# Stick-breaking attention tiles worked in their PSUM bank, without GpSimd

## The chip, the cores and the metric
The kernel runs on one core of a Trainium2 chip. The metric is the device time of one execution in microseconds (us). TensorE multiplies matrices, VectorE and ScalarE do elementwise work, GpSimd too, and SyncE starts the transfers. SBUF is the on-chip memory; PSUM holds the results of TensorE in eight banks of 512 fp32 columns by 128 partitions.

## The reference
Two blocks are run one after the other on a sequence of 512 tokens of width 1024. The first has a state-space layer, a latent-attention layer and a gated feed-forward after each. The second has two layers that project the input into three kinds of heads and gate and mix their outputs. The change touches the second block: the stick-breaking heads, and the rotation of the queries and keys of the differential heads.

```python
def _partial_rope(t, cos, sin):
    x1 = t[..., :half]; x2 = t[..., half:ROT_DIM]
    r1 = x1 * cos - x2 * sin
    r2 = x2 * cos + x1 * sin
    return jnp.concatenate([r1, r2, t[..., ROT_DIM:]], axis=-1)

# stick-breaking heads, one block of 128 queries
strict = kpos[None, :] < qpos[:, None]
z = jnp.einsum('bhqd,bhkd->bhqk', qb, k) * HEAD_DIM ** -0.5
log_fail = jnp.where(strict, jax.nn.log_sigmoid(-z), 0.0)
after = lax.cumsum(log_fail, axis=3, reverse=True) - log_fail
weights = jnp.where(strict, jnp.exp(jax.nn.log_sigmoid(z) + after), 0.0)
o = jnp.einsum('bhqk,bhkd->bhqd', weights, v)
```

## The kernel before
**Matrix products.** Most weights are fp32 and are split into a high and a low half of a faster format: ScalarE copies the raw weights into the high half (`wh`), VectorE subtracts to get the low half (`wl`); a product is then three matmuls. In the trace all tiles of a pool share a name: `wr_r`, `wh_r` and `wl_r` are raw, high and low weights; `bl` and `bh` hold the working tiles of the second block; `bank` is any PSUM bank; `x`, `xh_r`, `xl_r` are the hidden state and its halves.

**The order of work** is not the program order. The class `Plan` records every instruction of the whole kernel with an assumed cost, its dependences and a lag, and sorts them: a list scheduler runs forward and backward over all of the work twelve times and the order with the earliest modelled end is emitted. Each engine then executes its queue in that fixed order and waits where an operand is late. All instructions are issued from line 263, so every row of the trace names that line. The costs that matter here, in us for n columns (lines 175 to 197):

```python
t = 0.068 + n / 960.0                       # VectorE
if name == "tensor_scalar" and out.space != PSUM and n > 64 and ...:
    t = 0.12 + n / 1920.0                   # VectorE, all in SBUF
elif name == "affine_select":
    t = 0.05 + n * 0.0015                   # GpSimd
else:
    t = 0.15 + n * 0.0021                   # GpSimd, two tensors
```

**The second block's layer** (`block2_layer`) has 8 units of stick-breaking heads, then 16 of differential heads and 8 of forgetting heads. A unit is a pair of heads and a block of 128 queries. Between the units, as work for TensorE while the others run the elementwise steps, stand projections: queries, keys and values of later units (the table `before`, lines 2047 to 2053). During the units the banks are divided: two for projections (`g`), three for scores (`s`), two for transposes (`t`), one for outputs (`o`), each used in rotation.

A unit of stick-breaking heads (`attend_c`, line 1913) handles two heads (`e`). For each it multiplies queries and keys into a score bank, n = 128 to 512 columns, as far as the block's last key, and then makes the weights. With softplus(z) = max(z, ln(1 + exp(min(z, 30)))), a weight is the exponential of z minus the sum of softplus from the right up to its own column. Two GpSimd selects on the diagonal 128 columns keep the strict order: one sets softplus to zero there before the scan, one the weight after the exponential. The weights are transposed on TensorE, copied to SBUF and multiplied by the values.

The rotation (`roped`, line 1836) copies a projection out of its bank with a scale, exchanges rows by a VectorE shuffle, multiplies the exchanged copy by sines on GpSimd and the copy by cosines on VectorE, and adds. `split_q` and `split_k` then make high and low halves of queries and keys; for the differential heads' keys the subtraction in `split_k` runs on GpSimd.

Of the kernel before, what the change touches and what calls it, by code (L numbers as in the profile page):

```python
# [12 lines left out]
F32 = mybir.dt.float32  # L13
# [3 lines left out]
AF = mybir.ActivationFunctionType  # L17
ALU = mybir.AluOpType
AX = mybir.AxisListType

P = 128
D = 1024
S = 512
# [16 lines left out]
NEG = -1e30  # L40
# [486 lines left out]
class Net:  # L527
# [804 lines left out]

    def load_mask(self, pool):

        self.mask = pool.tile([P, S], F32, name="mask")
        self.nc.sync.dma_start(self.mask, self.A["mask"])

    def softmax_exp(self, e, p, i, sm):

        nc = self.nc  # L1340
        n = (i + 1) * P
        mx = self.small(1, "mx", 8)
        nc.vector.tensor_tensor_reduce(e[:, :n], p[:, :n], self.mask[:, S - n :], -1.0, 3e38, ALU.add, ALU.min, accum_out=mx)
        nc.scalar.activation(e[:, :n], e[:, :n], AF.Exp, scale=-1.0, bias=mx, accum_out=sm)
        return e

# [432 lines left out]
    def block2_layer(self, bp, l, hs, start):  # L1779
        nc, A = self.nc, self.A  # L1780
        V, G, SC = nc.vector, nc.gpsimd, nc.scalar
        wf, wv = A[f"w_in2f{l}"], A[f"w_in2v{l}"]
        tk = lambda: bp.tile([P, S], F32, tag="tk", bufs=7)
# [29 lines left out]
        def split_q(src, sc):  # L1813
            t = [qk(), qk()]
            for e, r in enumerate(halves):
                SC.activation(t[e][r], src[r], AF.Copy, scale=sc)
                V.scalar_tensor_tensor(t[e][halves[1 - e]], src[r], sc, t[e][r], ALU.mult, ALU.subtract)
            return t

        def split_k(src, E):  # L1820
            t, low = [qk(), qk()], [qk(), qk()]
            for e, r in enumerate(halves):
                for to in (r, halves[1 - e]):
                    SC.activation(t[e][to], src[r], AF.Copy)
                E.tensor_tensor(low[e][r], src[r], t[e][r], ALU.subtract)
                SC.activation(low[e][halves[1 - e]], low[e][r], AF.Copy)
            return t + low

        def scores2(q, k, e, i):
            n, d = (i + 1) * P, slice(i * P, (i + 1) * P)  # L1830
            p = self.psum("s")
            nc.tensor.matmul(p[:, :n], q[e][:, d], k[e][:, :n], start=True, stop=False)
            nc.tensor.matmul(p[:, :n], q[e][:, d], k[2 + e][:, :n], start=False, stop=True)
            return p

        def roped(name, j, sc):
            p = fm(name, j)
            x, sw = rk(), rk()
            SC.activation(x, p, AF.Copy, scale=sc)
            V.stream_shuffle(sw, x, [i + 8 if i < 8 else i - 8 if i < 16 else i for i in range(32)])  # L1840
            G.tensor_tensor(sw, sw, self.sin2, ALU.mult)
            V.tensor_tensor(x, x, self.cos2, ALU.mult)
            V.tensor_tensor(x, x, sw, ALU.add)
            return x

# [14 lines left out]
        qa, ka, qc, kc, qb, kb = ({} for _ in range(6))  # L1860
# [38 lines left out]
        def values(pr, i, pts, blk):  # L1899

            if i == 0:
                outs[pr] = self.psum("o")
            po = outs[pr]
            for j in range(i + 1):
                for e in range(2):
                    at = (2 * pr + e) * 64
                    nc.tensor.matmul(po[64 * e : 64 * e + 64, i * P : (i + 1) * P], vt[blk][:, j, at : at + 64],
                                     pts[e][:, j * P : (j + 1) * P], start=j == 0, stop=j == i,
                                     tile_position=(0, 64 * e))
            return outs.pop(pr) if i == NB - 1 else None  # L1910


        def attend_c(pr, i):
            n, d = (i + 1) * P, slice(i * P, (i + 1) * P)
            pts = []
            for e in range(2):
                p = scores2(qc[pr], kc[pr], e, i)
                z, sp = tk(), tk()
                SC.activation(z[:, :n], p[:, :n], AF.Copy)
                V.tensor_scalar(sp[:, :n], z[:, :n], 30.0, None, ALU.min)  # L1920
                SC.activation(sp[:, :n], sp[:, :n], AF.Exp)
                SC.activation(sp[:, :n], sp[:, :n], AF.Ln, bias=1.0)
                V.tensor_tensor(sp[:, :n], sp[:, :n], z[:, :n], ALU.max)
                G.affine_select(sp[:, d], sp[:, d], pattern=[[-1, P]], compare_op=ALU.is_gt, fill=0.0, base=0,
                                channel_multiplier=1)
                V.tensor_tensor_scan(sp[:, :n][:, ::-1], self.ones.to_broadcast([P, n]), sp[:, :n][:, ::-1], 0.0,
                                     ALU.mult, ALU.add)
                G.tensor_tensor(z[:, :n], z[:, :n], sp[:, :n], ALU.subtract)
                SC.activation(z[:, :n], z[:, :n], AF.Exp)
                G.affine_select(z[:, d], z[:, d], pattern=[[-1, P]], compare_op=ALU.is_gt, fill=0.0, base=0,  # L1930
                                channel_multiplier=1)
                pts.append(self.transp(bp, z, i, e))
            po = values(pr, i, pts, 3)
            if po is not None:
                V.tensor_tensor(gc[pr], po, gc[pr], ALU.mult)
# [95 lines left out]
            kc[1] = split_k(fm("ck", 1), V)  # L2031

        def aq(h):
            qa[h] = split_q(roped("aq", h, 0.125), 1.0)

        def ak(h):
            ka[h] = split_k(roped("ak", h, 1.0), G)

        def bk1():
            forget_k(1)  # L2040
# [2 lines left out]
            for h in range(4):  # L2043
                split_y(2 + h, ga[h])


        before = {0: [cq1], 1: [ck1], 2: [lambda: aq(0)], 3: [lambda: half_v(0)], 4: [lambda: ak(0)],
                  5: [lambda: half_v(0)], 6: [lambda: aq(1)], 8: [lambda: ak(1)], 9: [lambda: aq(2)],
                  10: [lambda: half_v(1)], 12: [lambda: ak(2)], 13: [lambda: half_v(1)], 14: [lambda: aq(3)],
                  16: [lambda: ak(3)], 17: [lambda: forget_q(0)],  # L2050
                  20: [lambda: half_v(2), lambda: forget_k(0)],
                  22: [lambda: half_v(2)], 24: [lambda: forget_q(1)],
                  25: [bk1]}
        units = [(attend_c, pr, i) for pr in range(2) for i in range(NB)]
        units += [(attend_a, h, i) for h in range(4) for i in range(NB)]
        units += [(attend_b, pr, i) for pr in range(2) for i in range(NB)]
# [83 lines left out]
def _layout(i):  # L2140
    f = np.float32
    a = {}
# [73 lines left out]
    cs[0:8] = cs[8:16] = np.cos(ang)  # L2216
    sn[0:8], sn[8:16] = -np.sin(ang), np.sin(ang)
    a["cos2"], a["sin2"] = np.concatenate([cs, cs]), np.concatenate([sn, sn])
    a["mask"] = np.where(np.arange(S)[None, :] - (S - P) <= np.arange(P)[:, None], 0, NEG).astype(f)
    a["ident"] = np.eye(P, dtype=f)  # L2220
    a["dmask"] = (np.arange(P)[:, None] % 16 == np.arange(16)[None, :]).astype(f)
    return {k: np.ascontiguousarray(v) for k, v in a.items()}
# [22 lines left out]
```

## Time and profile before

| | |
|---|---|
| median of 3 runs | 1873.94 us (1873.33 to 1874.26) |
| the profiled execution | 1873.71 us |
| its span, first to last instruction | 1871.9 us |
| TensorE / VectorE / ScalarE / GpSimd busy | 97% / 61% / 45% / 29% |
[...]
| chain that ended last, by engine | TensorE 76%, VectorE 9%, GpSimd 5%, ScalarE 4% |

The profile is of one execution. Busy times are unions of an engine's instructions; the time of a single instruction can overlap with the next one's. In the trace PE is TensorE, DVE VectorE, ACT ScalarE and POOL GpSimd. A wait is charged to the instruction that released it last.

### The profile page before, as it was taken

What the parts mean: (1) busy time and instruction counts of PE and PEld (TensorE: products, weight loads), DVE (VectorE), ACT (ScalarE), POOL (GpSimd) and SP (SyncE); (2) the same over time, 40 slices, a digit from 0 to 9 for tenths busy, and PEclk for the clock granted to TensorE, in tenths of its full rate; (3) what the DMA queues carried; (4) which work ended last, traced back from release to release, by engine and by line L of the source; (5) the groups of instructions that cost most, each with busy time, mean ns of one, the idle gap of its engine ahead of it and who ended that gap; (6) DMA issues with size and microseconds to landing.
All of it is one profiled execution on the core that took longest, in us unless ns stands there. A gap on an engine that the chain in (4) does not pass through costs nothing.

```text
span 1871.9 us, 27060 instructions
## 1 busy us (share of the span) xinstructions
PE 1809.5 (97%) x10296; PEld 1466.7 (78%) x10296; DVE 1151.0 (61%) x2222; ACT 838.9 (45%) x1572; POOL 551.1 (29%) x673
## 2 busy tenths in 40 slices
PE   7889999999999999999999999999899999989997
PEld 4667878888888777778888888987778788777877
DVE  8995364344345687755535444654888764478875
ACT  4224332222233577643212222435767643576764
POOL 5893121001012185321101101721632071154105
PEclk9999999999999999999999999999999999999999
DMA  4532333332333220023332332332121132211113
GB/s 132 143 90 88 94 95 100 92 101 84 104 91 93 91 74 12 13 87 99 91 101 91 90 102 87 121 108 80 34 68 58 57 113 85 82 35 60 58 57 113
DMA packets 73138, 157.88 MB, mean 84 GB/s; under 512 B 26416, under 2 KB 34864, under 8 KB 73008
## 3 DMA queue, kind: packets, MB, share of 16 engines
q1 hardware_dynamic: 73008, 156.15, 27.1%
q8 instruction: 81, 1.33, 0.3%
q14 instruction: 49, 0.40, 0.1%
HBM read 150.81 MB, written 4.72 MB: 83 GB/s over the span
## 4 chain that ended last, share of the span: by engine, by line
PE 76%; DVE 9%; POOL 5%; ACT 4%; issue 2%; DMA 1%; SPq 0%; ACTq 0%; DVEq 0%; POOLq 0%
PE bank L263 76%; DVE bl L263 3%; DVE s L263 2%; POOL x L263 2%; ACT bl L263 1%; DVE wl_r L263 1%; POOL bl L263 1%; POOL acc_r L263 1%; ACT bh L263 1%; DVE bank L263 1%; ACT wh_r L263 0%; DVE bh L263 0%; ACT xh_r L263 0%; DVE sm_r L263 0%; DVE xl_r L263 0%
## 5 line engine op out<-in xcount | busy, mean ns | idle before, releaser
L263 ACT ACTIVATE wh_r<-wr_r 128x1024 fp32r<-128x1024 f32 (+2 forms) x270 | 278.6, 1033 | 581.2 <-PE bank L263 529.0
L263 PE MATMUL bank<-xh_r,wl_r 128*128 128x512 f32 (+1 forms) x1312 | 502.9, 387 | 13.0 <-DVE wl_r L263 12.9
L263 PE MATMUL bank<-xl_r,wh_r 128*128 128x512 f32 (+1 forms) x1312 | 502.7, 387 | 0.6 <-DVE xl_r L263 0.5
L263 PE MATMUL bank<-xh_r,wh_r 128*128 128x512 f32 (+1 forms) x1312 | 501.3, 387 | 0.5 <-DVE s L263 0.5
L263 DVE TENSOR_TENSOR wl_r<-wr_r,wh_r 128x1024 fp32r<-128x1024 f32 (+2 forms) x270 | 372.4, 1380 | 155.5 <-ACT wh_r L263 149.7
L263 PEld LDWEIGHTS bank<-xh_r,wl_r 128*128 128x128 f32 x1312 | 248.2, 190 | 67.1 <-DVE wl_r L263 15.2
L263 PEld LDWEIGHTS bank<-xl_r,wh_r 128*128 128x128 f32 x1312 | 247.9, 189 | 53.2 <-issue 3.0
L263 PEld LDWEIGHTS bank<-xh_r,wh_r 128*128 128x128 f32 x1312 | 247.3, 189 | 52.8 <-issue 3.0
L263 POOL TENSOR_TENSOR ff<-ff,ff 128x512 f32<-128x512 f32 x44 | 62.6, 1422 | 590.2 <-DVE ff L263 575.0
L263 PE MATMUL bank<-ff,wh_r 128*128 128x512 f32 (+1 forms) x816 | 224.8, 363 | 0.2 <-ACT ff L263 0.2
L263 DVE TENSOR_TENSOR ff<-bank,ff 128x512 f32<-128x512 f32 x88 | 60.8, 691 | 224.0 <-PE bank L263 223.9
L263 PE MATMUL bank<-bh,wh_r 128*128 128x512 f32 (+1 forms) x656 | 178.4, 355 | 1.4 <-ACT bh L263 0.6
L263 PEld LDWEIGHTS bank<-ff,wh_r 128*128 128x128 f32 x816 | 145.3, 188 | 27.1 <-DVE ff L263 1.1
L263 PE MATMUL bank<-ff,wl_r 128*128 128x512 f32 (+1 forms) x408 | 146.4, 363 | 1.0 <-DVE wl_r L263 1.0
L263 DVE TENSOR_TENSOR x<-x,bank 128x256 f32<-128x256 f32 (+1 forms) x112 | 57.6, 531 | 129.9 <-PE bank L263 129.8
L263 PEld LDWEIGHTS bank<-bh,wh_r 128*128 128x128 f32 x656 | 113.2, 191 | 18.8 <-issue 2.6
L263 POOL TENSOR_TENSOR acc_r<-acc_r,sq_r 128x256 f32<-128x256 f32 (+1 forms) x63 | 75.4, 1198 | 158.4 <-ACT sq_r L263 158.2
L263 PE MATMUL bank<-bh,wl_r 128*128 128x512 f32 (+1 forms) x328 | 113.3, 355 | 1.4 <-DVE wl_r L263 1.4
L263 POOL TENSOR_TENSOR s<-s,s 128x512 f32<-128x512 f32 (+6 forms) x136 | 106.5, 815 | 24.6 <-DVE s L263 23.6
L263 ACT ACTIVATE ff<-ff 128x512 f32<-128x512 f32 x88 | 55.1, 626 | 74.4 <-POOL ff L263 68.8
L263 PEld LDWEIGHTS bank<-ff,wl_r 128*128 128x128 f32 x408 | 76.2, 188 | 13.7 <-DVE wl_r L263 1.2
L263 ACT ACTIVATE bl<-bank 128x256 f32<-128x256 f32 (+3 forms) x142 | 62.8, 453 | 49.8 <-PE bank L263 48.9
(257 smaller groups left out, 2803.5 us busy)
## 6 DMA issues: line engine op xcount, KB each, us to landing
wr_r<-w_gu SPq DMA_DIRECT2D x88, 512.0 KB, 3.5
wr_r<-w_in2f SPq DMA_DIRECT2D x48, 512.0 KB, 3.2
wr_r<-w_dn SPq DMA_DIRECT2D x37, 448.0 KB, 3.4
wr_r<-w_out SPq DMA_DIRECT2D x22, 512.0 KB, 3.2
wr_r<-w_dn SPq DMA_DIRECT2D x16, 512.0 KB, 3.5
wr_r<-w_in2v SPq DMA_DIRECT2D x16, 512.0 KB, 3.8
wr_r<-w_glu SPq DMA_DIRECT2D x12, 512.0 KB, 3.5
wr_r<-w_o SPq DMA_DIRECT2D x8, 512.0 KB, 3.2
```

The costliest lines, as they stand in the source:

```text
L263: lambda: f(*[real(v) for v in a], **{x: real(v) for x, v in k.items()}), load, rows, idle))
```

## The change
In `attend_c` the scores stay in their bank. A strict mask is added there to the diagonal 128 columns by VectorE: -1e30 where the key is not before the query. The mask is the causal mask of the softmax heads, loaded one column wider and read one column further on. The minimum, the maximum and the subtraction read the bank, the subtraction goes from GpSimd to VectorE, and both GpSimd selects and ScalarE's copy out of the bank are gone: with z at -1e30 softplus and weight come out as zero by themselves. In `roped` the cosine product reads the projection's bank instead of the copy; the scale of 0.125 goes from the copy to the split of the queries.

```diff
-        self.mask = pool.tile([P, S], F32, name="mask")
+        self.mask = pool.tile([P, S + 1], F32, name="mask")
...
-        nc.vector.tensor_tensor_reduce(e[:, :n], p[:, :n], self.mask[:, S - n :], -1.0, 3e38, ALU.add, ALU.min, accum_out=mx)
+        nc.vector.tensor_tensor_reduce(e[:, :n], p[:, :n], self.mask[:, S - n : S], -1.0, 3e38, ALU.add, ALU.min, accum_out=mx)
...
-        def roped(name, j, sc):
+        def roped(name, j):
             p = fm(name, j)
             x, sw = rk(), rk()
-            SC.activation(x, p, AF.Copy, scale=sc)
+            SC.activation(x, p, AF.Copy)
             V.stream_shuffle(sw, x, [i + 8 if i < 8 else i - 8 if i < 16 else i for i in range(32)])
             G.tensor_tensor(sw, sw, self.sin2, ALU.mult)
-            V.tensor_tensor(x, x, self.cos2, ALU.mult)
+            V.tensor_tensor(x, p, self.cos2, ALU.mult)
             V.tensor_tensor(x, x, sw, ALU.add)
             return x
...
             for e in range(2):
-                p = scores2(qc[pr], kc[pr], e, i)
-                z, sp = tk(), tk()
-                SC.activation(z[:, :n], p[:, :n], AF.Copy)
+                z, sp = scores2(qc[pr], kc[pr], e, i), tk()
+                V.tensor_tensor(z[:, d], z[:, d], self.mask[:, S - P + 1 :], ALU.add)
                 V.tensor_scalar(sp[:, :n], z[:, :n], 30.0, None, ALU.min)
                 SC.activation(sp[:, :n], sp[:, :n], AF.Exp)
                 SC.activation(sp[:, :n], sp[:, :n], AF.Ln, bias=1.0)
-                V.tensor_tensor(sp[:, :n], sp[:, :n], z[:, :n], ALU.max)
-                G.affine_select(sp[:, d], sp[:, d], pattern=[[-1, P]], compare_op=ALU.is_gt, fill=0.0, base=0,
-                                channel_multiplier=1)
+                V.tensor_tensor(sp[:, :n], z[:, :n], sp[:, :n], ALU.max)
                 V.tensor_tensor_scan(sp[:, :n][:, ::-1], self.ones.to_broadcast([P, n]), sp[:, :n][:, ::-1], 0.0,
                                      ALU.mult, ALU.add)
-                G.tensor_tensor(z[:, :n], z[:, :n], sp[:, :n], ALU.subtract)
-                SC.activation(z[:, :n], z[:, :n], AF.Exp)
-                G.affine_select(z[:, d], z[:, d], pattern=[[-1, P]], compare_op=ALU.is_gt, fill=0.0, base=0,
-                                channel_multiplier=1)
-                pts.append(self.transp(bp, z, i, e))
+                V.tensor_tensor(sp[:, :n], z[:, :n], sp[:, :n], ALU.subtract)
+                SC.activation(sp[:, :n], sp[:, :n], AF.Exp)
+                pts.append(self.transp(bp, sp, i, e))
...
-            qa[h] = split_q(roped("aq", h, 0.125), 1.0)
+            qa[h] = split_q(roped("aq", h), 0.125)
...
-            ka[h] = split_k(roped("ak", h, 1.0), G)
+            ka[h] = split_k(roped("ak", h), G)
...
-    a["mask"] = np.where(np.arange(S)[None, :] - (S - P) <= np.arange(P)[:, None], 0, NEG).astype(f)
+    a["mask"] = np.where(np.arange(S + 1)[None, :] - (S - P) <= np.arange(P)[:, None], 0, NEG).astype(f)
```

## Rows read from the trace of the kernel before

**Rows 1.** The page, busy us, share of the span, instructions.
```profile
PE 1809.5 (97%) x10296; PEld 1466.7 (78%) x10296; DVE 1151.0 (61%) x2222; ACT 838.9 (45%) x1572; POOL 551.1 (29%) x673
```

**Rows 2.** Windows: stretch, its us, each engine's busy us, clock, DMA share, GB/s.
```profile
1294.00:1371.00 77.00, 69.61 (x401) 54.08 (x400) 62.12 (x94) 53.19 (x113) 41.06 (x53) 0.98 0.18 56
1618.00:1695.00 77.00, 68.30 (x399) 53.19 (x397) 59.42 (x91) 52.75 (x113) 41.48 (x53) 1.00 0.18 58
1371.00:1500.00 129.00, 126.96 (x798) 105.62 (x797) 102.21 (x286) 86.74 (x197) 21.76 (x21) 1.00 0.18 57
1342.00:1372.00 30.00, 25.08 (x144) 19.00 (x144) 28.15 (x37) 21.19 (x39) 19.58 (x21) 0.94 0.21 66
```

**Rows 3.** Waits of PE, 1294 to 1695 us: total us, times, longest.
```profile
PE bank L263 <- POOL bl L263: 6.3, 7, 3.0
PE bank L263 <- DVE wl_r L263: 5.2, 4, 2.9
PE bank L263 <- ACT bl L263: 4.8, 7, 2.0
```

**Rows 4.** Timeline, 1354 to 1363 us: start, us, engine, instruction, idle before.
```profile
1356.02 3.46 DVE L263 TENSOR_TENSOR wl_r<-wr_r,wh_r 128x1024 fp32r<-128x1024 f32 x1
...
1357.14 1.25 POOL L263 TENSOR_TENSOR bl<-bl,bl 128x512 f32<-128x512 f32 x1
...
1359.53 0.80 PE L263 MATMUL bank<-xh_r,wl_r 128*128 128x512 f32 x1 [2.93 <-DVE wl_r L263]
...
1361.10 1.22 DVE L263 TENSOR_TENSOR_SCAN bl<-ones,bl 128x512 f32<-128x512 f32 x1
```

**Rows 5.** Groups by shape, VectorE, 1450 to 1500 us: busy us, mean ns, idle.
```profile
L263 DVE TENSOR_TENSOR wl_r<-wr_r,wh_r 128x1024 fp32r<-128x1024 f32 x5 | 6.1, 1218 | 0.7 <-ACT wh_r L263 0.7
L263 DVE TENSOR_TENSOR xl_r<-bh,xh_r 128x512 fp32r<-128x512 f32 x6 | 4.0, 684 | 0.7 <-ACT xh_r L263 0.7
...
L263 DVE COPY bl<-bank 128x512 f32<-128x512 f32 x2 | 1.4, 692 | 1.6 <-PE bank L263 1.5
...
L263 DVE COPY bl<-bank 128x256 f32<-128x256 f32 x2 | 0.8, 425 | 0.9 <-PE bank L263 0.8
L263 DVE COPY bl<-bank 128x128 f32<-128x128 f32 x2 | 0.6, 282 | 0.0
```

**Rows 6.** Windows: the 8 us around the wait of rows 4.
```profile
1358.00:1366.00 8.00, 6.47 (x28) 4.53 (x28) 7.90 (x9) 4.39 (x6) 5.95 (x6) 0.79 0.21 68
```

**Rows 7.** Groups by shape, VectorE, first stretch (1294 to 1371 us).
```profile
L263 DVE TENSOR_TENSOR wl_r<-wr_r,wh_r 128x1024 fp32r<-128x1024 f32 x9 | 13.2, 1467 | 8.7 <-ACT wh_r L263 8.7
L263 DVE TENSOR_TENSOR bl<-bl,bl 128x512 f32<-128x512 f32 x7 | 5.7, 831 | 0.5 <-ACT bl L263 0.4
L263 DVE TENSOR_TENSOR_SCAN bl<-ones,bl 128x512 f32<-128x512 f32 x4 | 5.7, 1435 | 0.4 <-POOL bl L263 0.4
...
L263 DVE SCALAR_TENSOR_TENSOR bh<-bl,bh 64x512 fp32r<-64x512 f32 x4 | 4.6, 1155 | 0.1
L263 DVE TENSOR_TENSOR bl<-bl,bh 128x512 f32<-128x512 f32 x3 | 3.3, 1092 | 0.0
...
L263 DVE TENSOR_SCALAR bl<-bl 128x512 f32<-128x512 f32 x4 | 2.4, 592 | 0.7 <-PE bank L263 0.7
```

**Rows 8.** Groups by shape, ScalarE, first stretch.
```profile
L263 ACT ACTIVATE bl<-bl 128x512 f32<-128x512 f32 x12 | 7.3, 624 | 2.8 <-POOL bl L263 2.7
...
L263 ACT ACTIVATE bl<-bank 128x512 f32<-128x512 f32 x10 | 5.7, 593 | 1.1 <-PE bank L263 1.0
```

**Rows 9.** Groups by shape, GpSimd, first stretch.
```profile
L263 POOL TENSOR_SCALAR_AFFINE_SELECT bl<-bl 128x128 f32<-128x128 f32 x32 | 15.8, 504 | 49.2 <-DVE bl L263 41.5 <-ACT bl L263 7.5
L263 POOL TENSOR_TENSOR bl<-bl,bl 128x512 f32<-128x512 f32 x4 | 6.8, 1706 | 1.2 <-DVE bl L263 1.2
...
L263 POOL TENSOR_TENSOR bl<-bl,bh 128x512 f32<-128x512 f32 x3 | 4.8, 1605 | 0.1
L263 POOL TENSOR_TENSOR bh<-bl,bh 64x512 fp32r<-64x512 f32 x2 | 4.2, 2094 | 0.1
```

## The prediction, made before the changed kernel was run
> **What bounds the kernel now.** I read the page's busy shares first [rows 1]: TensorE is busy 97% of the span, every other engine well below. So an edit to vector work can pay only where TensorE is kept waiting. I therefore cut the span into stages [rows 2]. The first two rows are the stretches of the stick-breaking heads, one for each layer of the second block, 77 us each; TensorE is busy 69.61 and 68.30 us there, so it idles 7.39 + 8.70 = 16.1 us. The third row is the rest of the attention of one layer: it idles only 2.0 of 129 us, with VectorE at 79%. In the fourth row, the tightest 30 us of the first stretch, VectorE is busy 28.15 us (94%) while TensorE stands still for 4.9 us. What the change can win lies in the two 77 us stretches, and VectorE is what may eat it.
>
> The waits of TensorE from the first stretch to the end of the second say who was late [rows 3]: GpSimd's part of a score tile 6.3 us, the low half of a split weight (a VectorE subtraction) 5.2 us, ScalarE's part of a tile 4.8 us. Together 16.3 us, which is the idle time of the two stretches.
>
> The longest wait for a weight, 2.93 us, can be followed in the timeline [rows 4]: the subtraction took 3.46 us, where the same one takes 1.218 us from 1450 to 1500 us, where GpSimd is all but idle [rows 5]. GpSimd's subtraction of the scores and one of its selects ran beside it. [...]
>
> So the two engines slow one another where they work at once. Against quiet prices [rows 5] the rows of the first 77 us [rows 7] are too long by: weight subtraction 9 x (1467 - 1218) = 2.2 us; the key's split 4 x (1155 - 684) = 1.9 us; cosine product 3 x (1092 - 684) = 1.2 us; sums and maxima of 512 columns 7 x (831 - 684) = 1.0 us; scans of 512, against the 1.22 us of one [rows 4], 4 x 0.215 = 0.9 us. Together 7.2 us of VectorE's 62.1.
>
> **The change, step by step.** A score tile has n = 128, 256, 384 or 512 columns; each width occurs four times a layer: 16 tiles a layer, 32 in all.
>
> *ScalarE:* the copy out of the bank goes, 593 ns at 512 columns [rows 8], scaled over the widths about 7 us a layer (an estimate) off an engine that is busy 53 of 77 us. It shortens the chain and is not the bound.
>
> *GpSimd:* both selects and the subtraction go, 32 selects at 504 ns and 1706 ns for a subtraction of 512 columns [rows 9]. Of its 41.06 us [rows 2] there stay the sine products and key splits, 4.8 + 4.2 = 9.0 us [rows 9], 22%.
>
> *VectorE, added:* the mask, 16 in-place additions of 128 columns in the bank. No row shows a step that reads and writes a bank; the nearest is a copy of 128 columns out of one, 282 ns [rows 5]. Below by that, above by twice it; I take the copy: 4.5 us (bound 9.0). The subtraction: priced as copies out of a bank, 692, 425 and 282 ns [rows 5] and for 384 columns the middle of its neighbours, 558: 1.96 x 4 = 7.8 us. The minimum reads the bank: 592 ns [rows 7] become 692 at 512 columns; I take 0.1 us for every width, 1.6 us. Sum 13.9 us a layer. The maximum keeps its size, one operand now from the bank.
>
> This rests on a bank being as quick to read as SBUF. The rows say so: 684 ns for a subtraction in SBUF, 692 ns for a copy out of a bank, both 512 wide [rows 5]. [...]
>
> *VectorE, given back:* 7.2 us are slowed-down time. 22% of GpSimd's work stays, so I take 5.6 us back; bounds 0 (if the long rows had another cause) and 7.2. Net 13.9 - 5.6 = +8.3 us: VectorE goes from 62.1 to 70.4 of 77 us, 91%. With nothing back it is 76.0 us, 99%.
>
> *The chain of one tile* of 512 columns, from scores to exponentials. Before: copy 0.59, minimum 0.59, two table steps at 0.62 [rows 8], maximum 0.83, select 0.50, scan 1.43, subtraction 1.71, exponential 0.62, select 0.50: 8.0 us. After: mask 0.28, minimum 0.69, 2 x 0.62, maximum 0.69, scan 1.22, subtraction 0.69, exponential 0.62: 5.4 us, with fewer hand-overs. Also, the kernel's own order of work, made from assumed costs, errs less: it books 1.23 us for a GpSimd subtraction that takes 1.71 and 0.24 for a select that takes 0.50, but 0.60 for a bank step that takes 0.69. TensorE waits where a step ends later than booked. The scan, booked at 0.60, stays wrong.
>
> *What comes free when.* A score tile holds its bank until the subtraction, 5.4 - 0.6 = 4.8 us at 512 columns instead of the 0.6 us of the copy; the rotary bank is held past the shuffle and the product, some 2 us by the same prices. There are three banks for scores and two for projections in these stretches. Behind a matmul that waits for a bank waits all of TensorE's queue.
>
> *Rotary product:* sixteen products at 1092 ns (beside GpSimd) become 0.69 us; three a stretch are counted above, the others lie where TensorE waits for nobody. The scale moves into a copy that is there anyway: nothing. The mask load is a column wider and far ahead of its use, beneath TensorE's matmuls: nothing.
>
> *Sum.* Waits for GpSimd, 6.3 us: the select is gone and the chain is 2.6 us shorter; a third may stay, as waits for the exponential: 4.2 us won. Waits for weights: of the 2.93 us, 3.46 - 1.22 = 2.2 us go, the rest stays. Waits for ScalarE, 4.8 us, stay. The clock's 1.3 us come back with the wait that they followed. Against this I set 1 us a layer of new waits, since VectorE goes to 91% and stood at 94% where TensorE idled most. 4.2 + 2.2 + 1.3 - 2.0 = 5.7 us. The profiled execution took 1873.71 us (span 1871.9), the median of the runs is 1873.94; 1873.7 - 5.7 = 1868.0.
>
> **The rivals.**
> *A, no net gain, 1873 us.* Waits for GpSimd become waits for VectorE of the same length: 8.3 us more of work a layer in the engine that the fourth row of [rows 2] shows full. Then 4.2 is lost again, and the clock's 1.3 too if one wait as long as 2.9 us remains: 1873.5. For it: that row. Against it: VectorE idles 15 us in the first stretch, mostly in its first half.
>
> *B, VectorE becomes the bound: slower, 1882 us.* If nothing is given back, it needs 76.0 us in a stretch. At the 94% of its tightest stretch this takes 80.9 us, 3.9 us beyond 77, 7.8 us over two layers: 1881.5. It decides once less than 13.9 - (0.94 x 77 - 62.1) = 3.6 us a layer come back. For it: the added steps have firm prices, the relief is inferred. Against it: the 3.46 us row.
>
> *C, the banks bind: 1873.7 + 5 = 1879 us.* The fourth tile's scores wait for the first's subtraction. Sixteen tiles in 77 us are 4.8 us apart, so three banks allow a hold of 14 us, where a tile needs 4.8 us and its queueing. Only in bursts, with tiles 2 us apart, would a hold of 7 us cost 1 us each; five such tiles a layer, half of it hidden, make +5 us in all. [...]
>
> *D, nearly all waits go: 1858 us.* 16.1 + 1.3 = 17.4 us is the most there is, 1856.3 the floor. For it: the chain is a third shorter. Against it: waits for weights and for ScalarE have causes that stay.
>
> **How the numbers follow.** Forecast 0.48 (its own range 1862 to 1871); A 0.24; B 0.15; C 0.05; D 0.08. A measurement tells 0.2%, 3.7 us, from no change. Faster: the forecast, D and a little of A, 0.57. Same: the rest of A, 0.23. Slower: B and C, 0.20. The range goes from D's time to just short of B's, 1858 to 1879; within it lies that the order is worked out for all of the kernel's work at once, so that the edit can shift it elsewhere.
>
> **What would show it.** Right: no wait of TensorE for GpSimd in the two stretches, weight subtractions near 1.22 us throughout, TensorE's idle time there down from 16.1 to about 10 us, the clock at 1.00, VectorE near 70 us a stretch. Wrong: waits on VectorE's steps above 10 us (A, B), score matmuls that wait for a subtraction (C), bank steps of 512 columns well above 0.7 us, or a difference outside these stretches.

## The result and the profile after
The changed kernel takes 1850.12 us (median of four runs, 1848.98 to 1850.94) against 1874.10 us (1873.33 to 1875.83) for the kernel before beside it: ratio 0.9866, interval 0.9854 to 0.9878. It is 24 us faster where 6 were forecast, and below the range of 1858 to 1879. The span of the profiled execution went from 1871.9 to 1849.2 us, 22.7 less.

The page's busy shares answer to [rows 1]; VectorE's total over the kernel hardly moves.

```profile
PE 1805.8 (98%) x10296; PEld 1466.8 (79%) x10296; DVE 1147.8 (62%) x2286; ACT 828.3 (45%) x1540; POOL 477.6 (26%) x577
```

The windows answer to [rows 2] and, in the last row, to [rows 6]: the two stretches, the rest of the attention of both layers, the 30 us that were tightest, and the 8 us of the lost clock.

```profile
1294.00:1371.00 77.00, 76.96 (x458) 61.70 (x456) 70.23 (x149) 55.73 (x114) 11.05 (x8) 1.00 0.18 62
1607.80:1684.80 77.00, 77.00 (x463) 62.24 (x462) 70.72 (x150) 55.66 (x113) 10.84 (x8) 1.00 0.19 62
1371.00:1490.00 119.00, 118.37 (x744) 98.80 (x745) 90.98 (x264) 79.30 (x180) 15.38 (x18) 1.00 0.18 59
...
1684.80:1801.00 116.20, 114.99 (x731) 96.95 (x730) 91.43 (x263) 79.10 (x182) 16.03 (x19) 1.00 0.19 60
1342.00:1372.00 30.00, 29.96 (x167) 22.76 (x167) 28.80 (x61) 24.40 (x50) 7.18 (x5) 1.00 0.22 71
1358.00:1366.00 8.00, 8.00 (x50) 6.23 (x49) 7.28 (x19) 5.54 (x12) 0.98 (x1) 1.00 0.40 131
```

TensorE idles 0.04 us in the two stretches together, where it idled 16.1, and VectorE is busy 70.2 and 70.7 us of 77, the 91% that was forecast, but with more work than was forecast: 149 and 150 steps, where the 94 and 91 of before and 32 added ones make 126 and 123. The rest belongs to work that came later before. In the 30 us in which TensorE stood still for 4.9 us beside a VectorE at 94%, it now stands still for 0.04 us beside one at 96%, which gets through 61 steps there instead of 37. The clock is 1.00 throughout. What remains of the attention idles 0.6 us in the first layer, where it idled 2.0, and 1.2 us in the second, where the kernel before idled 1.8:

```profile
1695.00:1823.60 128.60, 126.81 (x797) 105.98 (x797) 103.12 (x289) 86.39 (x198) 21.45 (x21) 1.00 0.17 57
```

So the idle time of both layers went from 19.9 us (16.1 + 2.0 + 1.8) to 1.9. That is 18.0 of the 22.7 us. Most of the rest is TensorE's busy time, 4.4 us less in the two layers; the 1.3 us of the clock are in it. Some of it goes with the waits. Matmuls of 512 columns in a row start 0.23 us apart while each shows 0.39 us, as these two of the kernel before do at the full clock:

```profile
1355.05 0.39 PE L263 MATMUL bank<-xh_r,wl_r 128*128 128x512 f32 x1
...
1355.28 0.39 PE L263 MATMUL bank<-xh_r,wh_r 128*128 128x512 f32 x1
```

Where TensorE stops, the last one ahead of the stop shows all of its 0.39 us: in the kernel before the one of 1356.20 us shows 0.40 ahead of the wait of 2.93. The two layers have 29 stops before and 10 after; 19 times 0.16 us make 3.0 us, as an estimate. The 0.80 us of the matmul in [rows 4] is no sign of this: the granted clock while it ran (1359.53 to 1360.33 us) was 0.51, then 0.50 to 1362.90 us, and 1.00 from 1363 to 1364 us.

The waits of TensorE from the first stretch to the end of the second layer (total, times, longest) answer to [rows 3]:

```profile
PE bank L263 <- POOL acc_r L263: 3.2, 1, 3.2
PE bank L263 <- DVE bl L263: 1.0, 2, 0.7
PE bank L263 <- ACT bh L263: 0.9, 2, 0.6
PE bank L263 <- ACT bl L263: 0.3, 2, 0.2
```

The 3.2 us are the norm between the layers and lie outside the attention. The three groups of [rows 3], 16.3 us, are down to 0.3 us for ScalarE; no wait for GpSimd's tiles or for a weight is left.

VectorE's groups by shape in the first stretch answer to [rows 7]:

```profile
L263 DVE TENSOR_TENSOR wl_r<-wr_r,wh_r 128x1024 fp32r<-128x1024 f32 x10 | 12.4, 1242 | 6.3 <-ACT wh_r L263 6.3
L263 DVE TENSOR_TENSOR bl<-bank,bl 128x512 f32<-128x512 f32 x8 | 5.3, 690 | 0.0
L263 DVE TENSOR_TENSOR_SCAN bl<-ones,bl 128x512 f32<-128x512 f32 x4 | 4.9, 1225 | 0.0
L263 DVE TENSOR_TENSOR bank<-bank,bh 128x128 f32<-128x128 f32 x16 | 4.4, 292 | 0.3 <-PE bank L263 0.2
...
L263 DVE TENSOR_TENSOR bl<-bl,bl 128x512 f32<-128x512 f32 x4 | 2.8, 688 | 0.0
L263 DVE SCALAR_TENSOR_TENSOR bh<-bl,bh 64x512 fp32r<-64x512 f32 x4 | 2.7, 686 | 0.2
...
L263 DVE TENSOR_SCALAR bl<-bank 128x512 f32<-128x512 f32 x4 | 2.7, 675 | 0.0
```

Each price came as forecast: mask 292 ns (282), maximum and subtraction from the bank 690 (692), weight subtraction 1242 (1218), scan 1225 (1220), key split 686 (684). In the second stretch the weight subtractions take 1351 ns in the mean: three of the ten are long, one of them 2.05 us beside a split that GpSimd keeps, but TensorE waits for none of them. Of GpSimd [rows 9], only the sine products and key splits are left, and the latter fell from 2094 to 1288 ns:

```profile
L263 POOL TENSOR_TENSOR bl<-bl,bh 128x512 f32<-128x512 f32 x4 | 5.9, 1476 | 81.1 <-DVE bl L263 61.9 <-ACT bl L263 10.5 <-PE bank L263 8.7
L263 POOL TENSOR_TENSOR bh<-bl,bh 64x512 fp32r<-64x512 f32 x4 | 5.2, 1288 | 6.2 <-ACT bh L263 6.1
```

A piece of the timeline (start, duration) shows VectorE's queue in the tight part:

```profile
1345.55 0.54 DVE L263 TENSOR_TENSOR bl<-bank,bl 128x384 f32<-128x384 f32 x1
...
1346.01 1.21 DVE L263 TENSOR_TENSOR wl_r<-wr_r,wh_r 128x1024 fp32r<-128x1024 f32 x1
...
1347.14 0.55 DVE L263 TENSOR_TENSOR bl<-bank,bl 128x384 f32<-128x384 f32 x1
```

Score steps and weight subtraction follow one another without a gap, each at its quiet price. The starts are 0.46 and 1.13 us apart for steps of 0.54 and 1.21: neighbours overlap by 0.08 us.

### The profile page after: what moved, and what is told of

It reads as the page before. It is cut to its first block, busy times and chain, and to the rows that moved or that the text cites. A ratio compares the mean times of both kernels' runs of the same rounds, so it can differ in the third digit from the quotient of the medians.

```text
span 1849.2 us, 26970 instructions
## 1 busy us (share of the span) xinstructions
PE 1805.8 (98%) x10296; PEld 1466.8 (79%) x10296; DVE 1147.8 (62%) x2286; ACT 828.3 (45%) x1540; POOL 477.6 (26%) x577
## 4 chain that ended last, share of the span: by engine, by line
PE 83%; DVE 5%; POOL 3%; ACT 3%; issue 1%; DMA 1%; ACTq 0%; SPq 0%; DVEq 0%; POOLq 0%
PE bank L263 83%; DVE s L263 2%; POOL x L263 2%; DVE wl_r L263 1%; ACT bl L263 1%; POOL acc_r L263 1%; ACT bh L263 1%; DVE bl L263 1%; ACT wh_r L263 1%; DVE bank L263 1%; DVE x L263 0%; ACT xl_r L263 0%; ACT xh_r L263 0%; DMA wr_r<-w_glu_a 0%; DMA mh<-w_kr 0%
## 5 line engine op out<-in xcount | busy, mean ns | idle before, releaser
L263 PE MATMUL bank<-bh,wh_r 128*128 128x512 f32 (+1 forms) x656 | 174.3, 352 | 0.9 <-ACT bh L263 0.6
L263 POOL TENSOR_TENSOR bl<-bl,bh 128x512 f32<-128x512 f32 x16 | 22.2, 1387 | 252.1 <-DVE bl L263 232.9
```

Source lines behind the costliest of these rows:

```text
L263: lambda: f(*[real(v) for v in a], **{x: real(v) for x, v in k.items()}), load, rows, idle))
```

## The experiments
Three explanations competed. *GpSimd's work was the loss*, either because its late steps stood in a tile's chain or because they slowed VectorE's steps beside them. *The bank is the gain*: no copy, fewer hand-overs. *The order is the gain*: the planner's list happened to come out better. In the expectations the first is theory 1 (1a: late steps, 1b: slowed steps), the second theories 2 and 3, the third theories 4 and 5. The prediction's rival C (banks held too long) and the scan's wrong booking were tried as well.

Two measures stand side by side: the time, and TensorE's idle time in the attention of both layers in the profiled execution (from the start of each stick-breaking stretch to the norm behind it). The order moves the first more than the second, as the first group of runs shows. All medians are set against the kernel before on the same chip.

| kernel | median us | ratio (95%) | TensorE idle, us |
|---|---|---|---|
| before | 1874.1 | | 19.9 |
| changed | 1850.1 | 0.9866 (0.9854 to 0.9878) | 1.9 |
| before, booking lower / higher | 1873.1 / 1872.1 | 1.0000 (0.9990 to 1.0010) / 0.9994 (0.9985 to 1.0003) | 19.5 / 16.3 |
| changed, booking lower / higher | 1858.7 / 1850.4 | 0.9924 (0.9907 to 0.9940) / 0.9873 (0.9857 to 0.9890) | 2.8 / 3.9 |
| stick-breaking part; booking lower | 1854.6; 1859.1 | 0.9904 (0.9889 to 0.9918); 0.9922 (0.9906 to 0.9939) | 7.0; 8.6 |
| rotary part; booking lower | 1861.3; 1870.4 | 0.9941 (0.9927 to 0.9956); 0.9978 (0.9969 to 0.9988) | 11.8; 13.5 |
| before, mask in SBUF | 1872.4 | 0.9993 (0.9983 to 1.0002) | 17.2 |
| before, subtraction on VectorE | 1861.2 | 0.9933 (0.9918 to 0.9948) | 9.8 |
| before, GpSimd booked as measured | 1866.3 | 0.9952 (0.9935 to 0.9969) | 13.4 |
| changed, in SBUF | 1857.1 | 0.9917 (0.9902 to 0.9932) | 7.0 |
| changed, loose scratch | 1852.9 | 0.9893 (0.9876 to 0.9909) | 1.9 |
| in SBUF, loose scratch | 1861.7 | 0.9932 (0.9917 to 0.9946) | 8.7 |
| changed, tied scratch | 1854.2 | 0.9901 (0.9886 to 0.9916) | 4.0 |
| in SBUF, tied scratch | 1879.3 | 1.0025 (1.0016 to 1.0035) | 17.8 |
| changed, two score banks | 1860.3 | 0.9926 (0.9911 to 0.9941) | 3.9 |
| changed, scan booked as measured | 1863.8 | 0.9947 (0.9930 to 0.9964) | 3.7 |

### Each part alone
The rotary product alone in the kernel before, and the changed kernel with the old rotation:

```diff
-            V.tensor_tensor(x, x, self.cos2, ALU.mult)
+            V.tensor_tensor(x, p, self.cos2, ALU.mult)
```

> The kernel before with the rotary part of the change alone (cosine product from the bank, scale moved to the split of the queries); the stick-breaking tiles are as before. Theory 1 (GpSimd's selects and subtractions in the chain of a tile are late, by their own length and by slowing VectorE beside them, and TensorE waits for what they hold up): 1872 to 1875 us, since all selects and subtractions are still there; the waits of TensorE for GpSimd stay at 5 to 7 us. Rival theory (the freed VectorE time of the sixteen cosine products is what counted): 1862 us or less.

> The stick-breaking part of the change alone; the rotation is as before. Theory 1: 1849 to 1853 us, the whole gain, and no wait of TensorE for GpSimd in the two stretches. Rival (the rotary part counts): 1860 us or more.

The stick-breaking part alone wins 19 us, the rotary part 12, more together than the 24 of both. Theory 1 had given all of the gain to the first and nothing to the second, so it missed both ranges. That called for a test of the order.

### The order shaken
The same programs with VectorE's booked cost in the second block moved by 8 ns, which changes only the list that the planner makes:

```diff
-            t = 0.068 + n / 960.0 + ...
+            t = 0.068 + self.jit + n / 960.0 + ...    # jit = -0.008 or 0.008
```

> The kernel before; only the assumed fixed cost of VectorE's steps in the second block is 0.008 us lower (0.060 for 0.068), so that its order of work comes out a little different; the same instructions. Theory 1 (the lateness is in the steps): the two layers together stay within 4 us of the kernel before, 1870 to 1877 us. Rival theory 5 (the gain or a part of it is a lucky order): the layers move by more than 5 us from this alone.

> As the run with the lower cost, with 0.008 us more (0.076). Theory 1: 1870 to 1877 us. Theory 5: more than 5 us away from the kernel before, up or down.

> The changed kernel with the assumed fixed cost of VectorE's steps in the second block 0.008 us lower; the same instructions in a slightly different order. Theory 1: 1847 to 1853 us, TensorE idle under 3 us in both layers. Theory 5: 1855 us or more.

> The changed kernel with the assumed fixed cost of VectorE's steps in the second block 0.008 us higher; the same instructions in another order. With the lower cost it took 1858.7 us. Theory 5 (up to some 9 us of the changed kernel's time hang on its order): anywhere from 1850 to 1860 us, and what moves is TensorE's waits in the two layers and the parts outside them. If the order of the changed kernel is as good as any: 1849 to 1852 us.

> The rotary part alone with the assumed fixed cost of VectorE's steps in the second block 0.008 us lower. The rotary part alone took 1861.3 us, where theory 1 expected 1872 to 1875. If its gain is an order that happens to be good (theory 5): 1868 us or more here. If it is the freed VectorE time or the later release of the projection bank itself: 1858 to 1865 us again.

> The stick-breaking part alone (rotation as before) with the assumed fixed cost of VectorE's steps in the second block 0.008 us lower; the same instructions. The part alone took 1854.6 us. If the part itself carries the gain and the order moves some microseconds: 1850 to 1861 us. If its gain were an order: 1866 us or more.

The kernel before stays within 2 us in three orders (the profiled execution of the lower booking was a long one, 1878.7 us; its idle time is read with that). The changed one spreads over 8.6 us, yet in each order it is at least 13 us faster than any of those three, and its idle time stays between 1.9 and 3.9 us. Its slow order has a span 7.9 us longer: 1.3 of them lie ahead of the layers, 1.1 behind them and 5.5 in them, where only 0.9 are idle time and the rest is TensorE at work, with some 40 matmuls more placed there. The rotary part falls from 11.9 us won to 4.2, so most of the time that it won alone was a lucky order. Its own effect is not nothing: alone it has 11.8 and 13.5 us of idle time where the kernel before has 16.3 to 19.9, and added to the stick-breaking part it takes idle time from 7.0 or 8.6 to between 1.9 and 3.9 us, and the time by 4.5 us in one pair and 0.3 in the other. With the stick-breaking part alone TensorE waits 4.3 us for VectorE's tiles (`bl`) in the two layers, 11 times, where it is 1.3 us before and 1.0 us with both parts: new waits for VectorE did come, and the rotary part took them away.

### GpSimd's steps one at a time
From the kernel before: the selects become a VectorE addition of the mask to the SBUF copy, the subtraction stays on GpSimd:

```diff
+                V.tensor_tensor(z[:, d], z[:, d], self.mask[:, S - P + 1 :], ALU.add)
-                G.affine_select(sp[:, d], sp[:, d], ...)
-                G.affine_select(z[:, d], z[:, d], ...)
```

> The kernel before with both selects replaced by one addition of the strict mask to the copied scores on VectorE; the subtraction stays on GpSimd, the copy on ScalarE. It takes 32 of GpSimd's 48 steps a layer out of the chain, 16 of its 32 us. Theory 1a (the chain waits for GpSimd itself): at least half of the 24 us, 1858 to 1862. Theory 1b (slowed VectorE): less than half, since the subtraction that stays reads two tiles and runs longest, 1863 to 1869.

The subtraction goes to VectorE, the selects stay:

```diff
-                G.tensor_tensor(z[:, :n], z[:, :n], sp[:, :n], ALU.subtract)
+                V.tensor_tensor(z[:, :n], z[:, :n], sp[:, :n], ALU.subtract)
```

> The kernel before with the subtraction moved to VectorE in SBUF; both selects stay on GpSimd. Theory 1a: the two selects still stand in the chain, 1860 to 1866 us. Theory 1b: the selects touch 128 columns only and slow little, 1855 to 1861 us. The order elsewhere differs from the kernel before, so the two stretches are read by themselves, not only the total.

Nothing moves, but the planner is told what the two steps take (in short):

```diff
-                t = 0.05 + n * 0.0015            # select
+                t = 0.50
-                t = 0.15 + n * 0.0021            # this subtraction
+                t = 0.05 + n * 0.0033
```

> The kernel before, with nothing changed on the engines; only the assumed costs by which the order is made are set to what the trace shows for the chain's GpSimd steps (a select 0.50 us, a subtraction 0.05 + 0.0033 n us). Theory 4 (TensorE waits because its order was made from too short costs): 1858 to 1864 us and few waits for GpSimd. If lateness that no cost can book (VectorE slowed, chain too long) is the cause: 1868 us or more. The order elsewhere differs, so the stretches are read by themselves.

Thirty-two selects a layer fewer win nothing, which neither theory's range allowed. VectorE's steps beside the remaining subtractions are slow, and TensorE's waits move on to ScalarE. Of this kernel, VectorE's groups in the first stretch, then TensorE's waits up to the end of the second:

```profile
L263 DVE TENSOR_TENSOR bl<-bl,bl 128x512 f32<-128x512 f32 x7 | 7.7, 1110 | 1.0 <-POOL bl L263 1.0
L263 DVE TENSOR_TENSOR_SCAN bl<-ones,bl 128x512 f32<-128x512 f32 x4 | 6.8, 1705 | 0.1
```

```profile
PE bank L263 <- ACT bl L263: 9.6, 8, 1.9
PE bank L263 <- DVE bl L263: 3.5, 6, 1.2
```

Sums and maxima take 1110 ns instead of 831 [rows 7], scans of 512 columns 1705 instead of 1435. The 16 subtractions a layer, which win 13 us when they leave, are the costly half. Of the kernel without them, TensorE's waits over the span of [rows 3]:

```profile
PE bank L263 <- POOL bl L263: 3.4, 7, 0.8
PE bank L263 <- ACT bl L263: 2.2, 4, 0.7
PE bank L263 <- DVE bl L263: 1.7, 2, 1.0
```

The 5.2 us of waits for a weight's low half are gone and those for ScalarE's tiles are halved, though neither step was touched. Booked rightly in place, GpSimd's steps win 8 us and a third of the idle time (13.4 us; the kernel before comes down to 16.3 in a shaken order): part of the loss was that the order trusted them.

### In the bank or in SBUF
The changed kernel with ScalarE's copy back, so that mask, minimum, maximum and subtraction work in SBUF:

```diff
-                z, sp = scores2(qc[pr], kc[pr], e, i), tk()
+                p = scores2(qc[pr], kc[pr], e, i)
+                z, sp = tk(), tk()
+                SC.activation(z[:, :n], p[:, :n], AF.Copy)
```

> The changed kernel, but the scores are copied out of the bank by ScalarE as before and mask, minimum, maximum and subtraction work on the copy in SBUF; no GpSimd step in the chain. Theory 1 (it is GpSimd's absence that counts): 1849 to 1855 us. Rival theory 2 (the chain is shorter because the copy is gone and ScalarE has 7 us a layer less): 1858 us or more. Rival theory 3 (steps that read the bank are not slowed by what is left of GpSimd's work): 1855 to 1860 us, with VectorE's steps in SBUF longer than their quiet times.

This kernel takes 1857.1 us, within what the order alone does to the changed kernel (1850.1 to 1858.7), and idles 7.0 us. That lies between the ranges of theories 1 and 2 and in that of theory 3, whose sign is absent: steps in SBUF have their quiet price (679 ns). So this run alone doesn't separate the bank from the order.

Then scratch work for GpSimd as before, whose result nobody uses: two selects and a subtraction for each tile, added to the changed kernel and to the SBUF one. It is first tied to nothing, then to the tile's transposed weights `pts[-1]`, so that it falls beside the later tiles' chains:

```diff
+                G.tensor_tensor(self.dum[:, :m], self.dum[:, :m], pts[-1][:, :m], ALU.subtract)
+                for _ in range(2):
+                    G.affine_select(self.dum[:, :P], self.dum[:, :P], ...)
```

> The changed kernel with GpSimd's work put back beside the chain: for every tile two selects of 128 columns and one subtraction (up to 480 columns) on a scratch tile that nobody else reads or waits for. The extra work changes no output. Theory 1a (late because the chain waits for GpSimd itself): 1850 to 1854 us. Theory 1b (late because GpSimd slows VectorE's steps beside it): 1858 to 1868 us, with weight subtractions and scans well above 1.22 us, although no step waits for the scratch work.

> The changed kernel with the tiles worked in SBUF as in the earlier run, and the scratch work of GpSimd put back beside the chain. Against the changed kernel with the same scratch work it shows whether reading the bank shields VectorE from GpSimd. Shield theory: 5 us or more slower than that kernel. No shield: within 3 us of it.

> The changed kernel with GpSimd's work put back beside the chain, this time tied to it: after each tile's weights are transposed and copied, one subtraction (up to 480 columns) reads that copy into a scratch tile and two selects follow on the scratch tile; no step of the kernel reads the scratch tile. In the earlier run of this kind the scratch work, tied to nothing, was done long before the stretch (GpSimd busy 18.4 us of 77, not 41), so it tested nothing. Theory 1b (GpSimd slows VectorE's steps beside it, and that makes TensorE wait): 1856 us or more. Theory 1a (only steps that the chain waits for count): 1849 to 1853 us, although weight subtractions and scans lengthen.

> The tiles worked in SBUF without GpSimd in the chain, and GpSimd's scratch work tied to each tile as in the second run of that kind. With the tiles in the bank the tied scratch work cost 4 us. Shield theory (steps that read the bank are not slowed by GpSimd, steps on two SBUF tiles are): 1866 us or more, minima, maxima and subtractions of 512 columns well above 0.69 us. No shield: 1857 to 1863 us.

The loose scratch ran ahead of the stretches (in the changed kernel GpSimd was busy 18 and 11 of 77 us there) and tested nothing but another order. Tied, it puts GpSimd at 41 to 43 us of 77, what the kernel before had [rows 2]. The windows of the two stretches, first the changed kernel with tied scratch, then the SBUF kernel without scratch, then with it:

```profile
1293.34:1370.34 77.00, 76.26 (x446) 60.06 (x445) 71.59 (x145) 53.62 (x108) 42.89 (x55) 1.00 0.18 62
1609.15:1686.15 77.00, 76.11 (x450) 60.61 (x449) 71.26 (x146) 53.36 (x110) 42.51 (x55) 1.00 0.18 62
```

```profile
1293.20:1370.20 77.00, 74.30 (x431) 59.21 (x431) 67.51 (x142) 56.66 (x122) 9.00 (x7) 0.98 0.18 62
1611.24:1688.24 77.00, 75.02 (x454) 60.28 (x454) 67.07 (x141) 56.37 (x122) 8.16 (x6) 1.00 0.18 62
```

```profile
1297.23:1374.23 77.00, 70.93 (x415) 55.76 (x414) 71.41 (x125) 54.37 (x114) 43.46 (x51) 1.00 0.17 56
1620.55:1697.55 77.00, 70.79 (x430) 56.77 (x429) 71.35 (x124) 53.64 (x114) 41.17 (x51) 1.00 0.17 56
```

The same scratch costs 4 us where the chain works in the bank, between the two ranges expected, and 22 where it works in SBUF, as the shield theory expected. In SBUF VectorE gets through 125 steps in 71.4 us where it did 142 in 67.5, 571 ns a step instead of 475, and TensorE idles 12.3 us of the two stretches. In the bank a step goes from 471 ns (70.23 us over 149) to 494. These means mix steps of different sizes; over both layers, where the steps are the same, VectorE's busy time rises by 24 us in SBUF (320.5 to 344.4) and by 6 in the bank (322.4 to 328.2). Of the 22 us, 4.0 lie ahead of the first of the two layers, which the edit doesn't touch, and are the order's; in idle time of the two layers the scratch costs 10.8 us against 2.1, while the order alone moved that by 3.6 at most. So the pair stands well outside what the order does.

Two other ways in which the scratch could delay the chain are alike in both kernels: GpSimd's own sine products and splits queue behind it, and it reads the transposed weights, whose three buffers come free later. The trace shows no more waits from either: VectorE waits 1.0 us for GpSimd's tiles in the layers of the SBUF kernel, 0.9 in the bank one and 0.9 in the changed kernel, TensorE and ScalarE not at all for a `bl` tile of GpSimd. Most of what TensorE waits for in the SBUF kernel with scratch is booked to ScalarE (first layer, then second):

```profile
PE bank L263 <- ACT bl L263: 5.7, 4, 2.5
...
PE bank L263 <- ACT bl L263: 5.7, 7, 1.8
```

VectorE's groups say which steps suffer. First the changed kernel with tied scratch, then the SBUF kernel, without and with it, first stretch:

```profile
L263 DVE TENSOR_TENSOR bl<-bank,bl 128x512 f32<-128x512 f32 x8 | 5.2, 673 | 0.0
L263 DVE TENSOR_TENSOR_SCAN bl<-ones,bl 128x512 f32<-128x512 f32 x4 | 4.9, 1236 | 0.0
...
L263 DVE TENSOR_TENSOR bl<-bl,bl 128x512 f32<-128x512 f32 x4 | 4.1, 1020 | 0.0
```

```profile
L263 DVE TENSOR_TENSOR bl<-bl,bl 128x512 f32<-128x512 f32 x12 | 7.9, 679 | 0.8 <-ACT bl L263 0.8
...
L263 DVE SCALAR_TENSOR_TENSOR bh<-bl,bh 64x512 fp32r<-64x512 f32 x4 | 2.7, 686 | 0.1
...
L263 DVE TENSOR_SCALAR bl<-bl 128x512 f32<-128x512 f32 x4 | 1.6, 411 | 1.1 <-PE bank L263 1.1
```

```profile
L263 DVE TENSOR_TENSOR bl<-bl,bl 128x512 f32<-128x512 f32 x11 | 9.7, 893 | 0.0
L263 DVE TENSOR_TENSOR_SCAN bl<-ones,bl 128x512 f32<-128x512 f32 x4 | 6.2, 1554 | 0.0
...
L263 DVE SCALAR_TENSOR_TENSOR bh<-bl,bh 64x512 fp32r<-64x512 f32 x3 | 3.9, 1316 | 0.1
...
L263 DVE TENSOR_SCALAR bl<-bl 128x512 f32<-128x512 f32 x4 | 2.8, 694 | 0.1
```

In one and the same kernel the steps with one operand in a bank keep their price beside GpSimd (673 ns; 690 without scratch), while the sums with both in SBUF go from 688 to 1020. With the chain in SBUF its own steps stretch: 679 to 893, the split 686 to 1316, the minimum 411 to 694. In these rows a VectorE step's loss beside GpSimd goes with where its operands lie; why, no run shows.

The scans of 512 columns in the first of the three fences look like an exception, 1236 ns with nothing in a bank. Single steps show how: the effect hangs on what GpSimd does just then. I take VectorE's steps with two inputs and at least 384 columns in the stretches of four traces (the kernel before, the changed one, both with tied scratch), as far as the timeline lists them singly. 58 with all operands in SBUF ran beside a product, split or subtraction of GpSimd for at least half of their quiet length: 35 of them took over 15% longer, up to 3.0 times, the others little or not at all. 42 with an operand in a bank did so too, and none took over 3% longer. And 26 in SBUF ran beside selects alone: none took over 15% longer. There it is the select that takes longer, as in the kernel before (start, duration):

```profile
1301.42 0.29 POOL L263 TENSOR_SCALAR_AFFINE_SELECT bl<-bl 128x128 f32<-128x128 f32 x1
...
1302.73 1.22 DVE L263 TENSOR_TENSOR wl_r<-wr_r,wh_r 128x1024 fp32r<-128x1024 f32 x1
...
1302.81 1.29 POOL L263 TENSOR_SCALAR_AFFINE_SELECT bl<-bl 128x128 f32<-128x128 f32 x1 [1.09 <-ACT bl L263]
```

The 13 selects of the two stretches that ran beside no VectorE step took 0.29 to 0.30 us, the 51 beside one 0.29 to 1.30; this one takes 1.29 and ends behind the weight subtraction, which keeps its 1.22. This fits that the selects' leaving wins nothing and the subtractions' leaving does.

### The bank hold and the scan
Two score banks instead of three, then the scan booked at its measured length (in short):

```diff
-self.banks(g=(0, 1), s=(2, 3, 4), t=(5, 6), o=(7,))
+self.banks(g=(0, 1), s=(2, 3), t=(5, 6), o=(7,))
```

> The changed kernel with two score banks in place of three, all else the same. It doubles the suspected cost of holding a bank through the chain (rival C of the prediction). If three banks were near binding: 1870 us or more, with score matmuls waiting for a VectorE subtraction. If the hold is far from binding: below 1860 us, within what the order alone moves.

```diff
-            t = 0.068 + n / 960.0                # scan
+            t = 0.16 + n / 1000.0 + n / 960.0
```

> The changed kernel with the scan booked in the order at what the trace shows (0.16 + n / 1000 + n / 960 us, 1.2 us at 512 columns, where 0.60 was booked); the same instructions. If the booked length still matters: 1846 to 1849 us, since the few waits that are left and the modelled end come from it. If TensorE waits for nobody in the stretches anyway: 1850 to 1859 us, as far as an order alone moves it.

With two banks TensorE's idle time rises by 2.0 us and the time by 10. The longest wait inside the layers stays under 1 us (rows: the waits of TensorE over both layers):

```profile
PE bank L263 <- ACT bl L263: 1.4, 4, 0.4
PE bank L263 <- DVE bl L263: 1.4, 4, 0.5
PE bank L263 <- ACT bh L263: 0.9, 1, 0.9
```

The 10 us are close to what a shaken order moves (8.6), so no price of a held bank can be read from them; that three banks don't bind is what the 0.04 us of idle time say. The truer scan gives no fewer waits and 14 us more time, with 5.5 of them ahead of both layers: another order. No version beat the changed kernel.

## Why the prediction was wrong
**Right.** What bounds the kernel and where most of the time could come from; every price of an added step; that VectorE's slow steps are relieved; the clock; GpSimd at 11 us a stretch (9.0 named). That a bank is as quick to read as SBUF, on which those prices rest, was borne out for two tensors of 512 columns: 690 ns from the bank, 688 in SBUF. For the minimum, which has one, it was not: 675 ns from the bank, 411 by itself in SBUF (the SBUF kernel without scratch); the 592 ns from which it was priced were slowed time.

**Right by luck: VectorE's 70 us.** The +8.1 us of the first stretch look like the +8.3 forecast, but 23 of its 55 more steps are work from later. Over the whole kernel VectorE's busy time falls by 3.2 us with 64 steps more. The stick-breaking part alone raises it by 3.9 us (1151.0 to 1154.9), 2 us a layer. So of the 13.9 us added a layer some 12 came back (an estimate from these totals), where the forecast took 5.6 and set 7.2 as the most: it counted the long rows of one stretch. One reading behind it is incomplete too: beside the 3.46 us subtraction of [rows 4] ran also GpSimd's key split (1354.98 us, 2.19 us long), which the change leaves.

**The step that failed is the sum.** It let a third of the waits for GpSimd (2.1 us), what was left of the waits for weights (3.0) and all waits for ScalarE (4.8) stand, and set 2.0 us of new waits for VectorE against the gain. In the stretches none stayed and none came: 2.1 + 3.0 + 4.8 + 2.0 = 11.9 us, which with the 5.7 makes 17.6. Those waits were treated as having causes of their own. The runs show that they hung for the most part on the same one: the subtraction's leaving alone halves the idle time (19.9 to 9.8 us), with no wait for a low half left and 2.2 us for ScalarE's tiles, and GpSimd scratch beside a chain in SBUF brings nearly all of it back (17.8) though no score tile goes through GpSimd; 11.4 us of that are booked to ScalarE, the last link of the chain. A releaser named in a wait can be the end of a late chain and not its cause.

**The second mistake is the worth of a busy share.** VectorE at 91% was charged with new waits because TensorE idled where VectorE stood at 94%. That 94% was itself stretched time: 37 steps filled it, where 61 now fill 96% and TensorE loses 0.04 us in 30.

**The floor.** "The most there is" counted 16.1 us in the stretches and 1.3 of clock. Outside it lay 1.9 us of idle time that went in the rest of the attention, and 3.1 us of TensorE's busy time. 17.4 + 1.9 + 3.1 = 22.4 of the 22.7 us. The rotary part, priced at nothing, has a share here: with the old rotation the layers idle 7.0 us, 5.3 of them outside the stretches, where the changed kernel idles 1.8. The 1.3 of clock, which the sum has too, are an estimate from [rows 6] (6.47 us of work at 0.79, times the 0.21 short of 1.00); no run shows the term by itself, and what the run shows in its place is 8.00 us of work at 1.00 in the same 8 us. Nor did every long wait go with a lower clock: behind the one of 3.03 us before 1692.27 us, in the kernel before, it was 1.00 up to 1696 us.

**The rivals.** D had the mechanism and was given 0.08; its size was bounded by that floor. A and B would have shown waits on VectorE's steps, and there are 1.0 us for its tiles. C is not seen with three banks.

**Open.** How much of the 24 us is a good order: one shaken order of the changed kernel wins 15, the other 24. How the rest divides between shorter chains, right booking and unslowed VectorE steps was not separated: taking the copy out (7.0 to 1.9 us idle) mixes chain and bank, and right booking alone took 6.5 of 19.9, in one order. That GpSimd's work beside steps in SBUF makes TensorE wait is shown by the pair with tied scratch; how much of the loss of the kernel before was this, and how much GpSimd's steps being late links of the chain, is not. Why a truer scan makes a worse list was not followed up.

## What to carry to other kernels
Before a wait is given a cause of its own, ask whether the steps ahead of it run at their quiet price; if two engines slow one another, the waits of a stretch may go together, as here, whichever engine they are booked to. Where GpSimd must do work on two tensors beside VectorE, try VectorE's steps with one operand in a bank: here those of 512 columns took 673 ns beside tied scratch, where sums with both in SBUF took 1020. Compare busy times only with the number of steps beside them. With an order made by a planner, shake the booked costs by a few ns and compare stalls as well as times before a part is credited: 11.9 us of a part alone shrank to 4.2.

## What was unexpected of the hardware
In these runs GpSimd's work beside VectorE costs by where VectorE's operands lie: sums of 512 columns with both in SBUF went from 688 to 1020 ns, steps with one in a bank stayed at 673 to 690. It costs by GpSimd's operation too: beside selects alone no step took over 15% longer, beside products, splits and subtractions up to 3.0 times. With GpSimd at 9 to 11 us of 77, the minimum by a constant over 512 columns is quicker in SBUF (411 ns) than out of a bank (675). An addition in place in a bank, 128 columns wide, takes 292 ns, about as much as a copy out of it (287), and successive VectorE steps overlap by about 0.08 us.
